# When an engine counts as free in the planner of a two-layer hybrid trunk

## The chip, the cores and the metric

The kernel runs on one core of a Trainium2 chip. The metric is the device time of one execution in microseconds (us). A core has five engines that run side by side, each through its own instructions in the order of the program: PE (TensorE, matrix products, with its weight loads, PEld), DVE (VectorE, elementwise work), ACT (ScalarE, functions and casts), POOL (GpSimd) and SP (SyncE, which here issues DMAs). They wait for one another through semaphores. So the program fixes the order on each engine, and the chip decides when each instruction runs.

## The reference

Two layers on 528 rows (512 tokens and 16 meta tokens put ahead) of 1024 features. A layer is a mixer and a feed-forward part, each with an RMS norm ahead and one behind, and a residual sum:

```python
def mixer_sublayer(h, pre_g, post_g, w_in, ...):
    u = rms_norm(h, pre_g)
    z = jnp.einsum("bld,de->ble", u, w_in)
    q, k, v, f_logit, a_val, a_gate, sc_b, sc_c, sc_x = jnp.split(z, idx, axis=-1)
    y_attn = forgetting_attention(q, k, v, log_f)          # 8 heads of 64, causal
    a = causal_depthwise_conv(a_val * sigmoid(a_gate), a_dw_w) + a_dw_b   # 31 taps
    y_conv = silu(layer_norm(a, a_ln_g, a_ln_b)) @ a_pw_w
    y_sc = sc_b * causal_depthwise_conv(sc_c * sc_x, sc_conv_w)           # 3 taps
    y = jnp.concatenate([y_attn, y_conv, y_sc], axis=-1)
    y = jnp.einsum("ble,ed->bld", head_rms_norm(y, head_g), w_out)
    return h + rms_norm(y, post_g)

def ffn_sublayer(h, pre_g, post_g, w_up, conv_w, w_down):
    z = causal_depthwise_conv(rms_norm(h, pre_g) @ w_up, conv_w)          # 3 taps
    g, up = jnp.split(z, 2, axis=-1)
    return h + rms_norm((silu(g) * up) @ w_down, post_g)
```

The feed-forward part has 2816 features inside. All is float32.

## The kernel before

Features lie on the 128 partitions, the 528 rows along the free axis, in two halves of 264. Each product of the weights is made of three matmuls of rounded parts (`mm3`, L618): high weight by high input, high by low, low by high. For it ACT casts a loaded weight block `raw` into `whi` and DVE subtracts to get `wlo` (L587 and L591 in planned code, L474 and L475 elsewhere); the inputs are split in the same way (`uhi`, `ulo`; `yhi`, `ylo`). A block has 8 slices of 128 inputs by 128 outputs, so a half of the rows needs 24 matmuls of it. The blocks are counted here in the order of use: W0 to W5 are the opening's, in mixer 0 the last are W21 (sc_x), W22 (sc_b), and then W23 and W24, the first two of w_out.

The stages, one after another: the opening (load of h, its norm, the first products), and for each layer the mixer, w_out with its post-norm, the FFN body, and ffn_down with its post-norm, behind which at the layer boundary lies the next pre-norm.

All stages but the FFN body are **planned in the source**: `Flow` (its `run` is printed below) is a list scheduler that runs while the program is built. Each piece of ACT, DVE, POOL or SP work is put in with `flow.op(engine, us, function, waits, prio)`, where `us` is a cost from a formula: `act_us(n) = 0.17 + 0.0009 n`, `dve_us(n) = 0.17 + 0.00101 n`, `stt_us(n) = 0.22 + 0.00102 n`. PE work comes from threads (generators), which count with `flow.mm(us)` and yield what they wait for. `run` keeps a clock `free[engine]` for each engine and one for PE. It always takes the piece that can start first; among those that an engine could start by then, the lowest `prio`, and then the one that was ready first. Only then is the instruction written into the program. So the times of the planner are used for nothing but the order.

The pieces of this order that matter below:

- **Norms.** Squares by ACT (L706, into `acc` or `c`), added by DVE (L715, `acc` plus `c`), summed over the partitions by PE with a constant matrix (L755, `acc` and `om_d`). ACT L765, L768, L769 and DVE L770, L776 make the factor. L797 or L1779 multiplies by it, ACT L799 or L1783 casts the result to `uhi`, DVE L800 or L1785 gives `ulo`. L832 and L842 scale the stage's output and add it to `h`. L731 is the square of the last output blocks.
- **Opening.** The first half's products run ahead of the norm (the factor comes in behind, by L893 to L901), the second half's wait for `uhi` and `ulo`.
- **Mixer.** Besides the attention (logits L1326 and L1372 with the maxima L1333, weighing L1418), DVE runs the 31 taps of the conv branch (L934). `conv_tail` (L1502 to L1546) then does its layer norm, silu and pointwise product. Each finished head block has a head norm: ACT squares, PE sums (L1100 for conv and short conv, L1484 for attention), ACT L1065, L1068, L1069, DVE L1070, L1073, L1084, then ACT L1087 `yhi` and DVE L1088 `ylo`. `conv_tail`, the projections W21 and W22 and the plain head norms take their psum banks from the ring "mm", which has two; a bank is taken again when the instructions that read it are planned as done:

```python
                ps, slot = yield from bank("mm")
                nc.tensor.matmul(ps[:, :H], lhsT=bd, rhs=sq[:, half_sl(hf)], start=True, stop=True)
                out.append(head_norm(i, yt, hf, ps[:, :H], slot, RMS_EPS, flow.mm(4 * mm_us(H))))
```

- **Early.** W23 and W24 start on those head blocks of `yhi`/`ylo` that are finished, while others are still on their way.
- **finish** does w_out or ffn_down: products in pairs of blocks, their evacuation (DVE L1610 adds the gathered product into `yp`, ACT L1613 scales it), squares, and the two norms.

## Time and profile before

| what | value |
|---|---|
| three runs, median (lowest to highest) | 1305.98 us (1305.32 to 1307.15) |
| profiled execution, its own time | 1305.24 us |
| its span | 1303.5 us |
| mean granted clock of TensorE | 0.994 |
| instructions | 24079 |
| DMA | 118.28 MB, 91 GB/s on average |

In a row of the profile stands the line of the kernel, the engine, the operation, the tile that is written and those that are read (buffer numbers left out), the shape, and a count. In a timeline the first two numbers are the start and the length, and brackets give the idle time of the engine just ahead and what ended it. In a row of a group, busy time and the mean of one instruction in ns stand behind the bar, and the idle time ahead. In a row of waits stand the total, the number of times and the longest. In a row of a window stand its length, each engine's busy time with its count of instructions (PE, PEld, DVE, ACT, POOL), the granted clock, the DMAs' share and GB/s. Matmuls are pipelined: one of 264 columns is shown 0.28 us long, and the next begins 0.12 us after it.

### The profile page before, as it was taken

The page shows a single profiled execution, that of the slowest core. Times are in us where ns is not written, and L with a number is a line of the kernel's source. Part 1 is how long each engine was busy: PE and PEld are TensorE (multiplying, and loading weights), DVE is VectorE, ACT ScalarE, POOL GpSimd, SP SyncE. Part 2 cuts the span into 40 slices and gives each one's busy share as a digit, 9 for nine tenths or more (in the row PEclk, how much of TensorE's full clock was granted, in tenths as well). Part 3 has the DMA queues.
Part 4 walks back from the last instruction along what each step waited for, and adds up shares of the span by engine and source line. Part 5 has one row for each costly group of instructions (what it writes and reads, how often), then busy time and mean ns, then how long its engine had stood idle before and what let it go on. Part 6 is the DMA issues. An engine that isn't in the chain of part 4 may idle for free. (4 is left out here: it accounts for less than half of the span.)

```text
span 1303.5 us, 24079 instructions
## 1 busy us (share of the span) xinstructions
PE 1274.5 (98%) x9922; PEld 1217.9 (93%) x9922; DVE 889.3 (68%) x1543; ACT 611.9 (47%) x1143; POOL 59.7 (5%) x166
## 2 busy tenths in 40 slices
PE   8999999999999999999989999999999999999997
PEld 8988888999999999999989898889999799989997
DVE  6888896687624663566677888856876256636664
ACT  6255567654423432344662565766543234314343
POOL 0311100000000000000003102100000000000000
PEclk8999999999999999999999999999999999999999
DMA  7133213502232223323330332234023332232221
GB/s 237 34 100 83 75 55 101 171 17 98 82 98 84 95 79 100 98 79 100 113 134 28 90 93 72 58 114 148 18 97 97 97 84 94 71 116 91 92 72 65
DMA packets 42798, 118.28 MB, mean 91 GB/s; under 512 B 4848, under 2 KB 15216, under 8 KB 42688
## 3 DMA queue, kind: packets, MB, share of 16 engines
q1 hardware_dynamic: 42640, 116.61, 28.6%
q8 instruction: 78, 1.28, 0.4%
q14 instruction: 32, 0.26, 0.1%
q0 software_dynamic: 48, 0.13, 0.0%
HBM read 108.04 MB, written 4.33 MB: 86 GB/s over the span
## 5 line engine op out<-in xcount | busy, mean ns | idle before, releaser
L618 PE MATMUL psum<-uhi,whi 128*128 128x264 f32 (+1 forms) x1936 | 453.4, 288 | 2.2 <-ACT uhi L799 1.1
L618 PE MATMUL psum<-ulo,whi 128*128 128x264 f32 (+1 forms) x1936 | 446.7, 285 | 1.0 <-DVE ulo L800 0.5
L618 PE MATMUL psum<-uhi,wlo 128*128 128x264 f32 (+1 forms) x1936 | 444.6, 283 | 0.0
L618 PEld LDWEIGHTS psum<-uhi,whi 128*128 128x128 f32 x1936 | 322.7, 189 | 4.7 <-ACT uhi L799 1.5
L618 PEld LDWEIGHTS psum<-ulo,whi 128*128 128x128 f32 x1936 | 323.9, 189 | 2.5 <-DVE ulo L800 0.7
L618 PEld LDWEIGHTS psum<-uhi,wlo 128*128 128x128 f32 x1936 | 323.5, 189 | 0.0
L618 PE MATMUL psum<-yhi,whi 128*128 128x264 f32 (+3 forms) x888 | 250.4, 305 | 7.4 <-ACT yhi L1087 2.9
L618 PE MATMUL psum<-ylo,whi 128*128 128x264 f32 (+3 forms) x888 | 247.6, 301 | 1.2 <-DVE ylo L1088 1.2
L618 PE MATMUL psum<-yhi,wlo 128*128 128x264 f32 (+3 forms) x888 | 247.3, 301 | 0.8 <-DVE wlo L591 0.8
L474 ACT CAST whi<-raw 128x1024 fp32r<-128x1024 f32 (+1 forms) x110 | 113.3, 1031 | 212.9 <-PE psum L618 199.3
L475 DVE TENSOR_TENSOR wlo<-raw,whi 128x1024 fp32r<-128x1024 f32 (+1 forms) x110 | 132.0, 1201 | 81.9 <-ACT whi L474 79.8
L618 PEld LDWEIGHTS psum<-yhi,whi 128*128 128x128 f32 x888 | 160.7, 190 | 15.7 <-ACT yhi L1087 4.3
L618 PEld LDWEIGHTS psum<-ylo,whi 128*128 128x128 f32 x888 | 161.2, 190 | 8.1 <-DVE ylo L1088 2.4
L618 PEld LDWEIGHTS psum<-yhi,wlo 128*128 128x128 f32 x888 | 161.1, 190 | 6.7 <-DVE wlo L591 1.4
L1885 DVE SCALAR_TENSOR_TENSOR c<-z,pv,c 128x528 f32<-128x528 f32 (+1 forms) x176 | 132.1, 757 | 2.7
L591 DVE TENSOR_TENSOR wlo<-raw,whi 128x1024 fp32r<-128x1024 f32 (+2 forms) x86 | 102.1, 1203 | 32.1 <-ACT whi L587 31.7
L587 ACT CAST whi<-raw 128x1024 fp32r<-128x1024 f32 (+2 forms) x86 | 87.6, 1032 | 27.1 <-PE psum L618 16.8
L934 DVE SCALAR_TENSOR_TENSOR cacc<-apad,pv,cacc 128x528 f32<-128x528 f32 x120 | 87.3, 762 | 0.8
L1903 ACT CAST yhi<-c 128x528 fp32r<-128x528 f32 (+1 forms) x44 | 27.6, 627 | 111.4 <-DVE c L1899 111.4
L1895 ACT ACTIVATE c<-c 128x528 f32<-128x528 f32 (+1 forms) x44 | 28.1, 639 | 81.8 <-DVE c L1885 81.8
L1848 DVE TENSOR_TENSOR z<-psum,rz 128x528 f32<-128x528 f32 x40 | 28.3, 708 | 53.8 <-PE psum L618 52.2
L1883 ACT ACTIVATE c<-z,pv 128x528 f32<-128x528 f32 (+1 forms) x88 | 63.3, 726 | 0.0
(214 smaller groups left out, 1364.0 us busy)
## 6 DMA issues: line engine op xcount, KB each, us to landing
raw<-in_w_dram SPq DMA_DIRECT2D x160, 512.0 KB
raw<-in_w_dram SPq DMA_DIRECT2D x32, 448.0 KB
h<-in_x_dram SPq DMA_DIRECT2D x16, 264.0 KB
raw<-in_w_dram SPq DMA_DIRECT2D x4, 528.0 KB
q<-q SPq DMA_DIRECT2D x16, 132.0 KB
k<-k SPq DMA_DIRECT2D x16, 132.0 KB
h_dram<-h SPq DMA_DIRECT2D x4, 528.0 KB
h<-h_dram SPq DMA_DIRECT2D x8, 264.0 KB
```

The costliest lines, as they stand in the source:

```text
L474: nc.scalar.copy(hi[:, :sz], raw[:, :sz])
L475: nc.vector.tensor_sub(lo[:, :sz], raw[:, :sz], hi[:, :sz].bitcast(F32))
L587: nc.scalar.copy(box["hi"][:, :sz], box["raw"][:, :sz])
L591: nc.vector.tensor_sub(lo[:, :sz], box["raw"][:, :sz], box["hi"][:, :sz].bitcast(F32))
L618: nc.tensor.matmul(d, lhsT=w[a][:, k, cols], rhs=rhs(b, k, hf), start=start and i == 0 and p == 0, stop=stop and i == n - 1 and p == 2)
L934: nc.vector.scalar_tensor_tensor(conv[j], in0=src, in1=conv[j], scalar=col("a_dw_w", CK * j + i), op0=ALU.mult, op1=ALU.add)
L1848: nc.vector.tensor_mul(two(t[:, off:]), srcs[0], two(rz))
L1883: nc.scalar.activation(dst, src[:, 2:2 + 2 * fw], AF.Copy, scale=wtap(2, t))
L1885: nc.vector.scalar_tensor_tensor(dst, in0=src[:, i:i + 2 * fw], scalar=wtap(i, t), in1=dst, op0=ALU.mult, op1=ALU.add)
L1895: silu = nc.scalar.activation(cs[0], cs[0], AF.Silu)
L1903: nc.scalar.copy(ghi, cs[0])
```

## The change

One line of `Flow.run`. After a piece is taken, its engine counts as free 0.09 us before the piece's result is there (never earlier than half its cost). The time of the result, `tok.time`, on which other pieces wait, is as before, and so is the cost of PE's work.

```diff
                 fn()
-                self.free[eng] = start + us
+                self.free[eng] = start + max(us - 0.09, 0.5 * us)
                 tok.time = start + us + lat
```

It holds for each planned engine: ACT, DVE, POOL, and SP, whose piece of 0.35 us for a DMA counts 0.26. No instruction is added or left out. What changes is the order in the planned stages: the planner sees ACT and DVE free earlier, by 0.09 for each piece since they were last idle, so that pieces change places, on PE too. Three places follow; the numbers in the names are buffer numbers.

**Opening, ACT.** The stretch from the casts of W1 and W2 to the first half's L765; the squares (L706) are those of the input `h`. Before:

```order
L587 CAST whi_224<-raw_183 128x1024
L587 CAST whi_236<-raw_191 128x1024
L706 ACTIVATE acc_243<-h_175 128x528
L706 ACTIVATE c_252<-h_175 128x528
L706 ACTIVATE c_260<-h_175 128x528
L587 CAST whi_271<-raw_208 128x1024
L706 ACTIVATE c_283<-h_175 128x528
L706 ACTIVATE acc_290<-h_175 128x528
L706 ACTIVATE c_299<-h_175 128x528
L706 ACTIVATE c_309<-h_175 128x528
L587 CAST whi_314<-raw_250 128x1024
L765 ACTIVATE rs_47_176<-psum_67,c_rms_102 128x264
```

And after:

```order
L706 ACTIVATE acc_218<-h_175 128x528
L587 CAST whi_227<-raw_183 128x1024
L587 CAST whi_238<-raw_188 128x1024
L706 ACTIVATE c_245<-h_175 128x528
L706 ACTIVATE c_254<-h_175 128x528
L706 ACTIVATE c_262<-h_175 128x528
L706 ACTIVATE acc_270<-h_175 128x528
L587 CAST whi_279<-raw_211 128x1024
L706 ACTIVATE c_288<-h_175 128x528
L706 ACTIVATE c_297<-h_175 128x528
L706 ACTIVATE c_299<-h_175 128x528
L765 ACTIVATE rs_47_176<-psum_67,c_rms_102 128x264
```

Before, the casts of W1, W2, W3 and W4 stand here, and the last square (into c) comes only behind L765. After, one square is ahead of W1, two more squares are ahead of W3, the last one is ahead of L765, and the cast of W4 has gone behind L765. On PE the first half's L755 comes behind 3 instead of 15 matmuls of W2, the second half's ahead of W3 instead of inside W4; on DVE the subtraction of W6 comes behind the second half's norm.

**End of mixer 0, DVE.** The last head norms ahead of w_out: `cacc` are the two conv head blocks, `sccx` is a short-conv head block. Before, the last twelve:

```order
L1073 SCALAR_TENSOR_TENSOR rs_t_2711<-rs_t_2711,rs_r_2710 128x264
L1084 SCALAR_TENSOR_TENSOR cacc_2544<-cacc_2544,pg_3_70,rs_t_2711 128x264
L1088 TENSOR_TENSOR ylo_293_2682<-cacc_2579,yhi_292_2681 128x264
L1088 TENSOR_TENSOR ylo_295_2694<-cacc_2544,yhi_294_2693 128x264
L1070 SCALAR_TENSOR_TENSOR rs_t_2734<-psum_67,rs_t_2734 128x264
L1073 SCALAR_TENSOR_TENSOR rs_t_2734<-rs_t_2734,rs_r_2733 128x264
L1070 SCALAR_TENSOR_TENSOR rs_t_2744<-psum_67,rs_t_2744 128x264
L1084 SCALAR_TENSOR_TENSOR cacc_2579<-cacc_2579,pg_3_70,rs_t_2734 128x264
L1073 SCALAR_TENSOR_TENSOR rs_t_2744<-rs_t_2744,rs_r_2743 128x264
L1084 SCALAR_TENSOR_TENSOR cacc_2544<-cacc_2544,pg_3_70,rs_t_2744 128x264
L1088 TENSOR_TENSOR ylo_293_2682<-cacc_2579,yhi_292_2681 128x264
L1088 TENSOR_TENSOR ylo_295_2694<-cacc_2544,yhi_294_2693 128x264
```

And after, the last ten:

```order
L1084 SCALAR_TENSOR_TENSOR cacc_2461<-cacc_2461,pg_3_70,rs_t_2625 128x264
L591 TENSOR_TENSOR wlo_2669<-raw_2207,whi_2659 128x1024
L1088 TENSOR_TENSOR ylo_288_2594<-cacc_2461,yhi_287_2593 128x264
L1070 SCALAR_TENSOR_TENSOR rs_t_2677<-psum_67,rs_t_2677 128x264
L1073 SCALAR_TENSOR_TENSOR rs_t_2677<-rs_t_2677,rs_r_2676 128x264
L1070 SCALAR_TENSOR_TENSOR rs_t_2685<-psum_67,rs_t_2685 128x264
L1084 SCALAR_TENSOR_TENSOR sccx_2158<-sccx_2158,pg_3_70,rs_t_2677 128x264
L1073 SCALAR_TENSOR_TENSOR rs_t_2685<-rs_t_2685,rs_r_2684 128x264
L1084 SCALAR_TENSOR_TENSOR sccx_2158<-sccx_2158,pg_3_70,rs_t_2685 128x264
L1088 TENSOR_TENSOR ylo_298_2664<-sccx_2158,yhi_297_2663 128x264 x2
```

Before, the two conv blocks come last; after, they are done, and the short-conv block is last. On PE the pointwise products and the conv head norms' L1100 come in front of W23 and W24, among W22's matmuls (15, 9 and 24 of them in a row), and L1100 of the short conv is last. The 31 taps end sooner on DVE, and W21 no longer runs among the maxima of the last two head pairs. Layer 1 has the same order as layer 0 now; before, it had another.

**Layer boundary, DVE.** The last pair of ffn_down of layer 0 (L1610), the second half's last square sum (L715), and the norm of the first half for layer 1. Before:

```order
L1610 TENSOR_TENSOR yp_2782<-yp_2782,psum_67 128x2x264
L770 SCALAR_TENSOR_TENSOR rz_2783<-psum_67,rz_2783 128x264
L776 SCALAR_TENSOR_TENSOR rz_2783<-rz_2783 128x264
L715 TENSOR_TENSOR acc_6985<-acc_6985,c_7329 128x528
L797 TENSOR_TENSOR yp_2782<-yp_2782,rz_2783 128x2x264 x4
L800 TENSOR_TENSOR ulo_108<-yp_2782,uhi_107 128x2x264 x2
```

And after:

```order
L770 SCALAR_TENSOR_TENSOR rz_2744<-psum_67,rz_2744 128x264
L776 SCALAR_TENSOR_TENSOR rz_2744<-rz_2744 128x264
L1610 TENSOR_TENSOR yp_2743<-yp_2743,psum_67 128x2x264
L797 TENSOR_TENSOR yp_2743<-yp_2743,rz_2744 128x2x264 x4
L715 TENSOR_TENSOR acc_6982<-acc_6982,c_7335 128x528
L800 TENSOR_TENSOR ulo_108<-yp_2743,uhi_107 128x2x264 x4
```

L1610 moves behind the factor (L770, L776), and L715 behind the four L797, which come ahead of it. On PE the L755 that reads this `acc` stands ahead of the first FFN product of the block behind, as before. In the tail of layer 1, L842 moves ahead of an L1610, and L755 of the last `acc` six matmuls forward.

## The prediction

> **What bounds the kernel now.** I read the page first (busy shares), then PE's waits, then the timelines of the places where PE waits. The page's first row and the heads of PE's list of waits:
>
> ```profile
> PE 1274.5 (98%) x9922; PEld 1217.9 (93%) x9922; DVE 889.3 (68%) x1543; ACT 611.9 (47%) x1143; POOL 59.7 (5%) x166
> ```
>
> ```profile
> PE psum L618 <- ACT yhi L1087: 2.9, 2, 1.5
> ...
> PE psum L755 <- DVE acc L715: 2.2, 1, 2.2
> PE psum L862 <- DVE yp L832: 1.4, 1, 1.4
> ```
>
> PE is busy 1274.5 of 1303.5 us, so 29 us is all that it waits in the whole span, and the change neither adds nor removes a matmul. The reader should see how little an order can win: the longest wait is 2.2 us, and most of the 29 us lies where one phase hands over to the next. What the change can do is to shift those hand-overs, in either direction. The profiled execution took 1305.24 us (span 1303.5, 1.74 around it); the three runs have a median of 1305.98, 0.74 more. I sum against the execution and add the 0.74 at the end.
>
> **Is the premise right?** The change lets the planner book an engine again 0.09 us before a result is there. Rows of the layer boundary, on DVE, then on ACT, each with the mean of one instruction of that group:
>
> ```profile
> 652.25 0.70 DVE L1610 TENSOR_TENSOR yp<-yp,psum 128x528 f32<-128x528 f32 x1 [1.22 <-PE psum L618]
> 652.87 0.42 DVE L770 SCALAR_TENSOR_TENSOR rz<-psum,rz 128x264 f32<-128x264 f32 x1
> 653.33 0.43 DVE L776 SCALAR_TENSOR_TENSOR rz<-rz 128x264 f32<-128x264 f32 x1
> 653.68 0.70 DVE L715 TENSOR_TENSOR acc<-acc,c 128x528 f32<-128x528 f32 x1
> 654.30 2.56 DVE L797 TENSOR_TENSOR yp<-yp,rz 128x528 f32<-128x528 f32 x4
> ```
>
> ```profile
> L797 DVE TENSOR_TENSOR yp<-yp,rz 128x528 f32<-128x528 f32 x8 | 5.2, 702 | 0.0
> ```
>
> ```profile
> 651.94 0.41 ACT L769 ACTIVATE rz<-rz 128x264 f32<-128x264 f32 x1
> ...
> 653.54 0.91 ACT L1613 ACTIVATE yp<-yp,pg 128x264 f32<-128x264 f32 x2
> ```
>
> ```profile
> L1613 ACT ACTIVATE yp<-yp,pg 128x264 f32<-128x264 f32 x16 | 7.5, 507 | 0.1
> ```
>
> Four L797 of 0.702 would be 2.81 one after another; they take 2.56, so each starts (2.81 − 2.56)/3 = 0.08 before the one ahead ends. Two L1613 overlap by 2 × 0.507 − 0.91 = 0.10. An instruction that reads the one ahead does not: L776 starts at 653.33, L770 ended at 653.29. So 0.09 is about the measured overlap on both engines, and results are still planned at their end. The planner's clock for a full DVE or ACT gets nearer to the chip's. But a nearer clock is no shorter chain: the instructions are the same and cost the same. The time can change only through the order, so I walk the new order by hand at the places where PE waits.
>
> **Term 1, the opening: −0.95 us.** The fence shows DVE on the way to the second half's input, and PE at its end.
>
> ```profile
> 24.33 0.43 DVE L776 SCALAR_TENSOR_TENSOR rz<-rs 128x264 f32<-128x264 f32 x1
> 24.68 1.25 DVE L591 TENSOR_TENSOR wlo<-raw,whi 128x1056 fp32r<-128x1056 f32 x1
> ...
> 27.35 0.43 DVE L770 SCALAR_TENSOR_TENSOR rs<-psum,rs 128x264 f32<-128x264 f32 x1 [0.74 <-ACT rs L769]
> ...
> 30.48 1.70 DVE L1779 SCALAR_TENSOR_TENSOR h<-h,pg,rs 128x264 f32<-128x264 f32 x4
> 32.09 0.70 DVE L1785 TENSOR_TENSOR ulo<-h,uhi 128x528 fp32r<-128x528 f32 x1
> ```
>
> ```profile
> 32.09 0.39 PE L618 MATMUL psum<-uhi,whi 128*128 128x264 f32 x1 [0.81 <-ACT uhi L1783]
> 32.85 0.39 PE L618 MATMUL psum<-ulo,whi 128*128 128x264 f32 x1 [0.37 <-DVE ulo L1785]
> ```
>
> PE has nothing from 31.28 (32.09 − 0.81), and loses 1.18. In the new order the squares go ahead of the weight casts, so that L755 of acc.0 stands 12 matmuls earlier and L755 of acc.1 27; the first half's factor (L776), at 24.76 before, can be there by about 23.4; the weight subtraction of 24.68 (1.25 long, 1.17 with the overlap) goes behind the norm. From 24.68 to 32.09 DVE takes 7.4 us, 0.9 of it idle. Without the subtraction, and with five more L1779 (1.61 from 30.48 to the next start, by four: 0.40 each) pulled ahead of the first ulo, that is 7.4 − 0.9 − 1.2 + 2.0 = 7.3: the first ulo could start at 23.4 + 7.3 = 30.7. I add 0.45 because L893 must wait for its product, so 31.15, and PE gets it 0.75 later, at 31.9 instead of 32.85. Gain 0.95; at most the 1.18 that is lost now, and nothing if L893 waits 1.4 longer than I think.
>
> **Term 2, the end of each mixer: +0.8 and +0.4 us.** This is the largest and least certain term. Before, the conv branch's head norms come last, and w_out waits for them. PE over the last part of mixer 0 as a window, then PE's waits in it, and two spacings after the same wait in layer 1:
>
> ```profile
> 170.55:222.66 52.11, 48.32 (x360) 42.70 (x359) 40.92 (x109) 36.42 (x101) 3.44 (x14) 1.00 0.26 83
> ```
>
> ```profile
> 216.70 0.39 PE L618 MATMUL psum<-ylo,whi 128*128 128x264 f32 x1 [0.39 <-DVE ylo L1088]
> ...
> 219.87 0.51 PE L618 MATMUL psum<-yhi,whi 128*128 128x264 f32 x2 [1.47 <-ACT yhi L1087]
> 220.64 0.39 PE L618 MATMUL psum<-ylo,whi 128*128 128x264 f32 x1 [0.26 <-DVE ylo L1088]
> ...
> 222.66 0.39 PE L618 MATMUL psum<-yhi,whi 128*128 128x264 f32 x1 [0.54 <-ACT acc L706]
> ```
>
> ```profile
> 868.45 0.61 PE L618 MATMUL psum<-yhi,whi 128*128 128x250 f32 x2 [1.47 <-ACT yhi L1087]
> 869.23 0.57 PE L618 MATMUL psum<-ylo,whi 128*128 128x250 f32 x1 [0.16 <-DVE ylo L1088]
> 869.60 0.41 PE L618 MATMUL psum<-yhi,wlo 128*128 128x250 f32 x1
> 869.81 0.41 PE L618 MATMUL psum<-ylo,whi 128*128 128x250 f32 x1
> ```
>
> Four waits, 0.39 + 1.47 + 0.26 + 0.54 = 2.66, stand at the end of mixer 0. They go: taps are done earlier on DVE, so conv_tail runs earlier, and the short-conv norms are last, behind the early products of w_out's first two blocks (W23, W24). But conv_tail, the sc_x and sc_b blocks (W21, W22) and the plain head norms all take their psum from the two "mm" banks, and now they come one behind another. A bank that a norm holds is free only when L1065, L1068, L1069 and L1070 are through:
>
> ```profile
> 216.91 0.48 ACT L1065 ACTIVATE rs_r<-psum,c_rms 128x264 f32<-128x264 f32 x1
> ...
> 217.60 0.41 ACT L1068 ACTIVATE rs_r<-rs_r 128x264 f32<-128x264 f32 x1
> 218.04 0.42 ACT L1069 ACTIVATE rs_t<-rs_r 128x264 f32<-128x264 f32 x1
> ```
>
> 0.48 + 0.41 + 0.42 and 0.43 for L1070 are 1.74, with four hand-overs of 0.05 some 1.95 us, in which PE has 9 to 15 matmuls of 0.12 (1.1 to 1.8 us) of W22 for cover at best, and sometimes a bank is missing for W22 itself. My walk finds new waits of 0.8 (the first pointwise product behind the silu chain), 1.9 (the fourth behind the copy that frees its bank, itself behind a weight cast on ACT), 2.7 (two L1100 and W22's second half behind the norms' banks) and 0.6 (W23 behind L1012): 6.0. It takes away the 2.66, about 2.0 in which lone norm matmuls stand wide apart (inside PE's busy time, so no row gives it), and 0.5 in the chain of the attention maxima: 5.2. Net +0.8 in layer 0. After the change layer 1 has layer 0's order; before, it lost 0.6 more than layer 0, because the matmuls from 869.60 on stand 0.21 apart where 0.12 is usual; so +0.4 there. The bounds: if the new waits are half as long, −2.2 and −2.6; if each of the four is a half longer, +3 each.
>
> **Term 3, the layer boundary: +0.55 us.** In the new DVE order L1610 goes behind L770 and L776, and L715 (acc with the last c) from ahead of the four L797 to behind them, while PE still has L755 of that acc ahead of the first FFN block. PE's rows:
>
> ```profile
> 654.44 1.16 PE L755 MATMUL psum<-acc,om_d 128*128 128x264 f32 x4 [2.23 <-DVE acc L715]
> 656.69 0.39 PE L618 MATMUL psum<-uhi,whi 128*128 128x264 f32 x1 [1.09 <-ACT uhi L799]
> 657.53 0.59 PE L618 MATMUL psum<-ulo,whi 128*128 128x264 f32 x1 [0.46 <-DVE ulo L800]
> 657.92 0.42 PE L618 MATMUL psum<-uhi,wlo 128*128 128x264 f32 x1
> 658.14 0.42 PE L618 MATMUL psum<-uhi,whi 128*128 128x264 f32 x1
> ...
> 660.34 0.34 PE L618 MATMUL psum<-ulo,whi 128*128 128x264 f32 x1
> ```
>
> L770 now comes first and starts at 652.38, since its factor by L769 ends at 652.35, L776 at 652.84, L1610 at 653.19, the L797 from 653.77 to 656.33, L715 to 656.95. PE's L755 goes at 657.05 instead of 654.44. Before, that L755 lay under the L797 and cost nothing; now it is in front of the first block, which starts at 657.95. Its third matmul comes at 658.4 where it came at 657.92: about +0.5. The idle time is one piece of 4.8, 652.21 (654.44 − 2.23) to 657.05, in place of 2.23 + 1.09 + 0.46. Already now the matmuls from 657.53 to 660.34 stand 0.22 apart instead of 0.12; that lasts to 3.65 us after 656.69. The same 3.65 from 657.05 ends at 660.7: +0.05 more. Bounds: 0 (L755 is done under the ulo) and +2 (the wide spacing lasts 13 matmuls longer, 13 × 0.1, and the 0.5).
> The Trainium skill, TensorE: Matmul & The Clock Gate, Part 1: The HAM clock gate, has the PE clock halved after an idle window of about 3.4 us and restored after as much busy time. The rows of the boundary agree (2.23 + 1.09 + 0.46 idle, 0.22 apart for 2.8 us). By that rule the 4.8 us in one piece costs what I put, and a bank wait of 1.9 costs no clock; but at 868.45 a single 1.47 was followed by the wide spacing, and in layer 0 the same 1.47 was not. So the rule alone does not settle the third rival below.
>
> **Costed at nothing.** In w_out and ffn_down casts and squares trade places, and PE has no wait there that these pieces end; if that cover went, each instruction that comes too late would show with its lateness. In the tail L842 goes ahead of L1610 and L755 of acc.15 six matmuls earlier (0.7 us): the input of its second part, c by L731, ends at 1288.71 (row below), and PE, which comes to it at 1289.56 now, at 1288.86, so no wait; the last chain, behind the last block's products, is unchanged.
>
> ```profile
> 1288.29 0.42 ACT L731 ACTIVATE c<-yp 128x256 f32<-128x256 f32 x1 [0.64 <-DVE yp L1632]
> ...
> 1289.56 0.59 PE L755 MATMUL psum<-c,om_d 128*128 128x256 f32 x2
> ```
>
> SP's loads and POOL's memsets swap by a place or a few; the loads run far ahead of use. Bounds for all this: −0.5 to +0.5.
>
> **Sum.** −0.95 + 0.8 + 0.4 + 0.55 + 0 = +0.8: 1306.0 for such an execution, 1306.8 with the 0.74 to the median. A measurement tells about 0.2% (2.6 us) from no change.
>
> **Rivals.**
> *The banks do not bind* (chance 0.27). The conv branch finishes early, as the DVE rows intend, and half the 6.0 of new waits is hidden: mixers −2.2 and −2.6, the rest as above: 0.8 − 1.2 − 4.8 = −5.2 to the execution, 1300.8. For it: 2.66 is at stake in rows, and DVE is 40.92 of 52.11 busy in the window, so it has room. Against it: only two banks, and a holding time near 2 us each.
> *Slower through PE's clock* (0.28). The bank waits come in pieces long enough that the matmuls behind them stand 0.22 apart, 13 of them at each mixer end (13 × 0.1 = 1.3, as from 869.60 on), and the boundary's 4.8 us adds its further 1.5: 1306.8 + 1.3 + 1.3 + 1.5 = 1310.9. It decides once a wait before w_out is over about 1.5 us. For it: layer 1 shows it after 1.47. Against it: layer 0 does not.
> *Nothing comes through* (0.12). PE is 98% busy; the moved instructions are under its cover, and gains and losses are each under a microsecond: 1306.0.
> My forecast has the rest, 0.33, with its own range of 1304.5 to 1309.
>
> **How the numbers follow.** Faster by over 0.2% (under 1303.4) holds nearly all of the first rival and a little of the forecast: 0.27. Slower (over 1308.6) holds most of the second and the forecast's upper end: 0.30. The rest, 0.43, is within. The range reaches to the first rival's 1300.8 less 0.8, and to the second's 1310.9 plus 0.6: 1300 to 1311.5 leaves about a tenth on each side.
>
> **What would show it.** Opening: PE's wait for uhi L1783 and ulo L1785 of 1.18 falls to about 0.3. Mixers: no wait for yhi L1087 of the conv norm just before w_out, but waits of L1100, L1531's followers and W22 for L1070 or for L1546's copy. Boundary: one wait of L755 for acc L715 of about 4.8 us. The prediction is wrong if PE's list of waits shows under 3 us of bank waits in both mixers together (then the first rival), or if the granted clock falls at the mixer ends (the second). It would be wrong in its premise if the FFN body, which is not planned, changed by more than 0.3 us.

## The result: 1.5% slower, and where the time went

| kernel | median, us (lowest to highest) | ratio to before, 95% interval |
|---|---|---|
| before | 1306.05 (1305.32 to 1307.15) | |
| after | 1326.26 (1324.57 to 1327.81) | 1.015 (1.0137 to 1.0164) |

The forecast was 1306.8, its range 1300 to 1311.5. The change costs 20.2 us. In the profiled execution the span is 22.3 us longer, 1325.8 in place of 1303.5. The page's first row after the change:

```profile
PE 1286.5 (97%) x9922; PEld 1225.4 (92%) x9922; DVE 887.0 (67%) x1543; ACT 611.4 (46%) x1143; POOL 58.9 (4%) x166
```

The work is the same. PE is shown 12 us busier because a matmul at a lower clock is shown longer (0.42 instead of 0.29 us in the rows below). So the busy row hides half of the loss, and I compared the stages by milestones instead: the starts, in PE's timeline, of matmuls that occur once or in few groups. "Attention part" runs from the sums of the forget gate (L1211) to the fourth and last weighing (L1418), "mixer's end" from there to the first square sum behind w_out (L755). That L755 shifts by a few matmuls between orders, so a difference under half a microsecond means nothing, and one at a mixer's end holds up to 1 us of it (8 matmuls in layer 0).

| stage | before, us | after, us | difference | forecast |
|---|---|---|---|---|
| start to L1211 of mixer 0 | 72.0 | 69.9 | −2.1 | −0.95 |
| attention part, layer 0 | 120.1 | 127.1 | +7.0 | 0 |
| mixer's end, layer 0 | 57.2 | 63.3 | +6.1 | +0.8 |
| first w_out and FFN, layer 0 | 386.4 | 389.0 | +2.6 | 0 |
| layer boundary to L1211 of mixer 1 | 82.6 | 83.1 | +0.5 | +0.55 |
| attention part, layer 1 | 121.0 | 123.7 | +2.7 | 0 |
| mixer's end, layer 1 | 58.3 | 63.8 | +5.4 | +0.4 |
| second w_out, FFN, to the tail | 379.3 | 379.3 | 0 | 0 |

Almost all of it lies in the two mixers: 9.7 in their attention parts and 11.5 at their ends. The border between the two is not firm, since the new order moves work across it: after the change 18 and 15 fewer matmuls of L618 stand in the attention parts, and 24 and 21 more at the ends. At 0.12 us each this is an estimate of what equal work costs more: 9.2 and 4.5 in the attention parts, 3.2 and 2.9 at the ends. The whole mixers are 13.1 and 8.1 us longer. The waits of PE after the change, the longest ones and what answers to those shown of before:

```profile
PE psum L1100 <- DVE rs_t L1070: 4.1, 2, 2.0
PE psum L755 <- DVE acc L715: 4.1, 1, 4.1
PE psum L1326 <- ACT yta L1448: 3.6, 2, 2.2
PE psum L618 <- DVE wlo L591: 2.5, 3, 1.0
...
PE psum L862 <- DVE yp L832: 1.4, 1, 1.4
...
PE psum L1100 <- DVE sccx L1012: 1.2, 2, 0.6
```

The wait for the conv norm's yhi (L1087) is gone, as forecast, and norm sums (L1100) that wait for a bank to be freed by L1070 are new, as forecast too. The L1326 that wait for L1448 are new, and I did not foresee them: they stand in the attention part.

**Mixer's end.** PE where the two conv norms queue:

```profile
211.39 0.29 PE L618 MATMUL psum<-uhi,wlo 128*128 128x264 f32 x1
212.30 1.13 PE L1100 MATMUL psum<-apad,bd 128*128 128x264 f32 x4 [0.61 <-DVE sccx L1012]
215.46 1.25 PE L1100 MATMUL psum<-apad,bd 128*128 128x264 f32 x2 [2.04 <-DVE rs_t L1070]
216.27 0.66 PE L618 MATMUL psum<-uhi,whi 128*128 128x264 f32 x1
216.73 0.42 PE L618 MATMUL psum<-ulo,whi 128*128 128x264 f32 x1
216.95 0.42 PE L618 MATMUL psum<-uhi,wlo 128*128 128x264 f32 x1
```

Between 211.39 and 216.27 the PE gets three norm sums done. Behind the wait the next matmuls stand 0.22 apart instead of 0.12: the clock had fallen. Its granted value, the third number from the right, in three windows of 5 us:

```profile
140.00:145.00 5.00, 5.00 (x32) 4.84 (x31) 3.27 (x10) 0.71 (x2) 0.00 (x0) 0.67 0.31 102
190.00:195.00 5.00, 5.00 (x27) 4.83 (x28) 4.28 (x13) 2.22 (x6) 1.43 (x4) 0.66 0.00 0
215.00:220.00 5.00, 4.54 (x24) 4.23 (x25) 3.97 (x10) 2.83 (x8) 0.00 (x0) 0.66 0.00 0
```

Each such window loses about a third of 5 us, 1.7 us; before, no window of mixer 0 was below 1.00. Over all 5 us windows up to PE's last matmul, what the clock lacks to 1.00 sums to 11.9 us after and 6.9 before, 5.0 of the 22 us. By stage the difference is larger in the mixers: 8.5 after and 1.7 before in the two of them together, while the opening lacked 3.4 before and nothing after. This bounds what the clock can have cost, since it also counts time in which PE waits.

**Attention part.** DVE in the middle of it, after:

```profile
112.80 0.44 DVE L1333 CUSTOM_DVE_ANT_0 junk<-psum,causal 128x272 bf16<-128x272 f32 x1
...
113.16 0.77 DVE L934 SCALAR_TENSOR_TENSOR cacc<-apad,pv,cacc 128x528 f32<-128x528 f32 x1
113.85 0.57 DVE L1333 CUSTOM_DVE_ANT_0 junk<-psum,causal 128x400 bf16<-128x400 f32 x1
...
114.56 0.43 DVE L1333 CUSTOM_DVE_ANT_0 junk<-psum,causal 128x264 bf16<-128x264 f32 x1
...
117.18 0.77 DVE L934 SCALAR_TENSOR_TENSOR cacc<-apad,pv,cacc 128x528 f32<-128x528 f32 x1
117.86 0.43 DVE L1073 SCALAR_TENSOR_TENSOR rs_t<-rs_t,rs_r 128x264 f32<-128x264 f32 x1
118.21 0.77 DVE L934 SCALAR_TENSOR_TENSOR cacc<-apad,pv,cacc 128x528 f32<-128x528 f32 x1
...
126.61 2.45 DVE L591 TENSOR_TENSOR wlo<-raw,whi 128x1024 fp32r<-128x1024 f32 x2
...
132.28 1.22 DVE L591 TENSOR_TENSOR wlo<-raw,whi 128x1024 fp32r<-128x1024 f32 x1
```

Taps of the conv branch (L934) stand among the maxima and the factors of the head norms. The subtraction of W15 comes at 126.61 and that of W17 at 132.28; before they came at 115.98 and 128.65:

```profile
115.98 1.22 DVE L591 TENSOR_TENSOR wlo<-raw,whi 128x1024 fp32r<-128x1024 f32 x1
...
128.65 1.22 DVE L591 TENSOR_TENSOR wlo<-raw,whi 128x1024 fp32r<-128x1024 f32 x1
```

A subtraction frees one of three buffers into which later weights are loaded, and SP issues the loads in order. Two of the three are held by W18 and W19, which are loaded and not yet cast, so the load of the conv branch's pointwise weight (the first of four in these rows) can go only when W17's subtraction is through. SP's queue after, then before:

```profile
133.53 29.05 SPq L583 DMA_DIRECT2D raw<-in_w_dram  x4
```

```profile
129.89 25.29 SPq L583 DMA_DIRECT2D raw<-in_w_dram  x4
```

So this weight lands later, and ACT, whose next instruction is its cast, waits 6.01 us for that transfer (4.16 before), with the evacuation of a weighing (L1445 to L1449) behind it. ACT after, then before:

```profile
137.12 0.62 ACT L587 CAST pw<-raw 128x512 fp32r<-128x512 f32 x1 [6.01 <-DMA raw<-in_w_dram]
137.65 0.59 ACT L1445 ACTIVATE s<-psum 128x512 f32<-128x512 f32 x1
...
138.69 0.18 ACT L1448 COPY yta<-psum 128x16 f32<-128x16 f32 x1
```

```profile
132.58 0.62 ACT L587 CAST pw<-raw 128x512 fp32r<-128x512 f32 x1 [4.16 <-DMA raw<-in_w_dram]
```

PE needs the bank that L1448 frees. It has no such wait before. Its row after:

```profile
138.93 0.50 PE L1326 MATMUL psum<-k,q 128*128 128x144 f32 x2 [2.23 <-ACT yta L1448]
```

And the early taps brought nothing. The last one before started at 171.52, the last one after at 142.45, yet conv_tail's first product starts later. The last tap and conv_tail after, then before:

```profile
142.45 0.76 DVE L934 SCALAR_TENSOR_TENSOR cacc<-apad,pv,cacc 128x528 f32<-128x528 f32 x1
```

```profile
182.01 1.94 PE L1502 MATMUL psum<-cacc,om_c 128*128 128x264 f32 x8
```

```profile
171.52 0.76 DVE L934 SCALAR_TENSOR_TENSOR cacc<-apad,pv,cacc 128x528 f32<-128x528 f32 x1
```

```profile
174.21 0.61 PE L1502 MATMUL psum<-cacc,om_c 128*128 128x264 f32 x2
```

The thread of conv_tail is started at its own place in the list of projections (`fill`), right behind the second sc_c block (W19), whose last matmul is at 181.88. The finished taps lay 39 us.

A switch in the program decides where the taps go: of 31 taps a block, the first 25 have priority 4, the last `LATE = 6` have 0.5, ahead of head norms (1) and weight subtractions (2).

```python
            for i in range(CK):
                for j in range(2):
                    last[j] = dve(stt_us(L), lambda j=j, i=i: tap(j, i), last[j], prio=4 if i < CK - LATE else 0.5)
```

The planner's own clock (numbers of the program, not of the chip) has the first tap of priority 0.5 at 153 us in the kernel before and at 104 us in the changed one, since a DVE that is free 0.09 us earlier after each instruction takes a tap into more gaps. With the cut on DVE alone it is 121, so the cut on ACT has its part in it. Below, "late taps from" is this number.

### The profile page after: what moved, and what is told of

It reads as the page before. It is cut to its first block, busy times and chain, and to the rows that moved or that the text cites. A ratio compares the mean times of both kernels' runs of the same rounds, so it can differ in the third digit from the quotient of the medians.

```text
span 1325.8 us, 24082 instructions
## 1 busy us (share of the span) xinstructions
PE 1286.5 (97%) x9922; PEld 1225.4 (92%) x9922; DVE 887.0 (67%) x1543; ACT 611.4 (46%) x1143; POOL 58.9 (4%) x166
## 5 line engine op out<-in xcount | busy, mean ns | idle before, releaser
L618 PE MATMUL psum<-uhi,whi 128*128 128x264 f32 (+1 forms) x1936 | 460.0, 290 | 2.2 <-DVE rs_t L1070 1.0
L618 PE MATMUL psum<-ulo,whi 128*128 128x264 f32 (+1 forms) x1936 | 452.1, 286 | 0.9 <-DVE ulo L1785 0.6
L618 PE MATMUL psum<-uhi,wlo 128*128 128x264 f32 (+1 forms) x1936 | 449.9, 284 | 0.0
L618 PEld LDWEIGHTS psum<-uhi,whi 128*128 128x128 f32 x1936 | 326.5, 190 | 5.3 <-DVE rs_t L1070 1.9
L618 PEld LDWEIGHTS psum<-ulo,whi 128*128 128x128 f32 x1936 | 327.4, 190 | 2.2 <-DVE ulo L1785 0.8
L618 PEld LDWEIGHTS psum<-uhi,wlo 128*128 128x128 f32 x1936 | 327.0, 190 | 0.0
L618 PE MATMUL psum<-yhi,whi 128*128 128x264 f32 (+3 forms) x888 | 249.1, 303 | 3.7 <-ACT whi L587 2.3
L618 PE MATMUL psum<-yhi,wlo 128*128 128x264 f32 (+3 forms) x888 | 246.4, 300 | 2.5 <-DVE wlo L591 2.5
L618 PE MATMUL psum<-ylo,whi 128*128 128x264 f32 (+3 forms) x888 | 245.9, 299 | 0.0
L618 PEld LDWEIGHTS psum<-yhi,whi 128*128 128x128 f32 x888 | 160.1, 189 | 11.1 <-ACT whi L587 3.0
L618 PEld LDWEIGHTS psum<-yhi,wlo 128*128 128x128 f32 x888 | 160.0, 189 | 8.5 <-DVE wlo L591 3.2
L618 PEld LDWEIGHTS psum<-ylo,whi 128*128 128x128 f32 x888 | 160.3, 189 | 5.5
L934 DVE SCALAR_TENSOR_TENSOR cacc<-apad,pv,cacc 128x528 f32<-128x528 f32 x120 | 87.2, 762 | 0.7
L1848 DVE TENSOR_TENSOR z<-psum,rz 128x528 f32<-128x528 f32 x40 | 28.3, 707 | 52.9 <-PE psum L618 51.4
L1883 ACT ACTIVATE c<-z,pv 128x528 f32<-128x528 f32 (+1 forms) x88 | 63.3, 726 | 0.4 <-DVE z L1851 0.4
```

Of the source, the lines that this page charges most:

```text
L618: nc.tensor.matmul(d, lhsT=w[a][:, k, cols], rhs=rhs(b, k, hf), start=start and i == 0 and p == 0, stop=stop and i == n - 1 and p == 2)
L934: nc.vector.scalar_tensor_tensor(conv[j], in0=src, in1=conv[j], scalar=col("a_dw_w", CK * j + i), op0=ALU.mult, op1=ALU.add)
L1848: nc.vector.tensor_mul(two(t[:, off:]), srcs[0], two(rz))
L1883: nc.scalar.activation(dst, src[:, 2:2 + 2 * fw], AF.Copy, scale=wtap(2, t))
```

## The experiments

The theories by their letters, as the expectations use them: A, the cut on DVE is to blame (A', because some lines of DVE get an early start that they do not have); B, the cut on ACT; C, the order of SP's loads; D, the rival to all, that any change of the planner's numbers spoils a finely fitted order; E, the late taps; F, the queue for two psum banks at the mixers' ends, my forecast's own mechanism; G, E and F together.

The kernels differ from the one before in the lines shown. Where there is no diff of the planner's line, it is that of the change. All times are medians in us; before was 1305.9 to 1306.6 beside them.

### One engine at a time, and one stage at a time

```diff
-                self.free[eng] = start + us
+                self.free[eng] = start + (max(us - 0.09, 0.5 * us) if eng == "dve" else us)
```

e1_dve is this; e2_act has `eng == "act"`, e3_sp_pool `eng in ("sp", "pool")`, and in e4_outside the condition is a flag that is off while a mixer is planned.

> The cut of 0.09 for DVE alone; ACT, POOL and SP are planned as before. Theory A (the planner runs ahead of the chip on DVE: it puts low-priority taps and square sums into DVE time that isn't there, so the attention chain and the weight subtractions come late, and with them loads): most of the 20 us comes from DVE, 1318 to 1328 us, and a mixer longer by over 6 us. Theory B (the cut on ACT is what hurts): within 3 us of before. Theory C (SP's loads trading places with the q and k copies hurts): within 5 us of before. Theory D (any small change of the planner's numbers throws a finely fitted order off): 1310 to 1325 as for the other engines.

> The cut for ACT alone. Theory A: within 5 us of before (1301 to 1311), since ACT is busy 47% and seldom the engine that is waited for. Theory B: 1316 to 1326. Theory C: within 5 us. Theory D: 1310 to 1325.

> The cut for SP and POOL alone. Theory A and B: within 2 us of before. Theory C: a large part of the 20 us, 1314 to 1324, with the load of the pointwise weight landing some 4 us later than before. Theory D: 1308 to 1320.

> The cut on all engines, but not while the two mixers are planned: it holds in the opening, in w_out and in ffn_down with their norms. Theory A: the mixers as before, the opening 1.4 us faster, w_out and the boundary slower by up to 3.5: 1303 to 1309. Theory D: the order of the mixers starts from another state and is thrown off all the same, 1310 to 1320. If the loss lies outside the mixers, 1318 or more.

Measured: DVE alone 1305.24, ratio 0.9991 (0.998 to 1.0002); ACT alone 1308.9, 1.0022 (1.001 to 1.0033); SP and POOL alone 1306.19, 1.0001 (0.999 to 1.0013); outside the mixers 1306.14, 0.9997 (0.9986 to 1.0008). Theory A, that the cut on DVE is to blame by itself, fell at once: it costs nothing. B and C fell as well, though ACT alone costs 3.0 us, with an end of mixer 0 of 65.8 us. The loss needs the mixers, and no engine alone gives it. In e4_outside the stage from the first w_out on was 389.1, as after the change: that 2.6 belongs to the cut in w_out, and the opening's gain sets off part of it. D had its first counts against it: three changes of the planner in four cost nothing.

### Both engines, mixers alone, and the late taps

f3_dve_act and f4_mixers are the condition `eng in ("dve", "act")` and the flag the other way round. The other two touch only the switch:

```diff
 # f1_late0: the change, and
-LATE = 6
+LATE = 0
 # f2_before_late: no change of the planner, and
-LATE = 6
+LATE = 15
```

> The changed kernel (cut on every engine), but with LATE = 0: the last six taps of each conv block keep priority 4 and never rank ahead of a head norm (1) or a weight subtraction (2). Theory E (the cut makes the taps run ahead in the plan, so that their last six, of priority 0.5, reach the attention chain some 55 us sooner and push the weight subtractions W15 to W17 and the head norms back): 1304 to 1312. Theory D (any change of the planner's numbers costs): 1315 to 1330. Theory C (loads behind the q and k copies): 1320 to 1330.

> The kernel before, without any cut, but LATE = 15, so that priority 0.5 begins at the same place of the attention chain as in the changed kernel (the planner's 101 us; 104 in the changed kernel, 153 before). Theory E: slower by 6 to 20 us, 1312 to 1326, without any cut. Theories A, B: within 4 us of before. Theory D: 1310 to 1325 too, so only f1 tells E from D.

> The cut for DVE and ACT together, SP and POOL planned as before. If SP's order is part of the loss (theory C, in company with the others): under 1318. Theory E: the taps reach priority 0.5 at the same place (the planner's 104 us), so 1322 to 1330.

> The cut on every engine, only while the two mixers are planned, the complement of the run outside the mixers. If the stages add up: 1326. Theory E: the planner reaches priority 0.5 at 116 us, between the changed kernel (104) and the cut on DVE alone (121, 1305): between 1305 and 1326, some 1315.

Measured: f1 1319.87, 1.0104 (1.0075 to 1.0134); f2 1324.1, 1.0137 (1.0107 to 1.0166); f3 1326.36, 1.0154 (1.0124 to 1.0183); f4 1324.71, 1.0141 (1.0112 to 1.0171). DVE and ACT together are the whole loss, though each alone is none or little of it. f2 costs 18 us with no cut at all: its late taps begin at 101, and nine more taps of each block have the priority. Its attention parts are 125.4 and 125.8, its ends 64.0 and 63.8. But it is not the changed kernel's loss over again: PE has no wait of L1326 for L1448 in it, waits longest for L1012 (5.1 in two waits), and its granted clock is 0.56, 0.50 and 0.58 in the three windows from 125 to 140 us. f1 gave back only 6.4, which lies in D's range and not in E's: its attention parts fell to 123.4 and 122.6, its ends stayed long (63.6 and 61.3). In f1 the subtraction of W15 is back at 117.0, yet that of W17 comes at 132.6, ACT still waits 5.83 for the pointwise weight and PE 2.04 for L1448. So the last six taps are not what delays that load; what does is open. Theory E, the late taps, is at most half of an answer, and the mixers' ends are another matter. f4 came out longer than my guess, near the sum of the stages (1326).

### Other banks for the head norms, and truer costs

```diff
 # g1_cut_acc (with the change) and g2_acc (without), in plain_head_norm
-                ps, slot = yield from bank("mm")
+                ps, slot = yield from bank("acc")
                 nc.tensor.matmul(ps[:, :H], lhsT=bd, rhs=sq[:, half_sl(hf)], start=True, stop=True)
```

In h1_exempt the cut does not hold for the 64-partition subtractions and the maxima, which I took to have no early start on the chip (for the maxima the trace bears this out only where another maximum follows, see the last section): for `eng == "dve"` and the pieces of L1259, L1287 and L1333 the engine is booked for `us + 0.04`. g3_cut03 has 0.03 in place of 0.09.

> The changed kernel, but the plain head norms (L1100) take their psum bank from the ring acc, which is idle after the last weighing, instead of mm. Theory F (the mixer's end is longer by some 6 us in each layer because conv_tail, W22 and the norms queue for two mm banks, and PE's clock falls behind the waits): 1313 to 1319, with the waits of L1100 for L1070 (4.1 us now) under 1 us. If the banks are not the cause of the mixer's end: 1322 to 1330. The attention part stays as in the changed kernel in both.

> The kernel before, without a cut, with the same other ring for the head norms. Theory F: its norms come behind the first blocks of w_out and do not queue in front of W22, so little changes, 1303 to 1308. It is also the yardstick for the run before it.

> The cut on every engine, except on three lines of DVE whose next instruction does not start early on the chip: the 64-partition subtractions L1259 and L1287 (next start 0.03 us after the end) and the maxima L1333 (some 0.2 us after): those count 0.04 us more than their cost. Theory A' (the plan is too early for DVE in the attention part because these 200 instructions get a cut that they do not have, so taps are squeezed in ahead of time that is not there): the attention part as long as before, 1306 to 1315, the taps' priority 0.5 from the planner's 132 us on. Theory D (any change throws the order off): 1315 to 1330.

> A cut of 0.03 instead of 0.09 on every engine. Theories A', E and F, by size: the plan runs ahead by a third as much, so 1306 to 1313. Theory D: as likely 1315 to 1325 as less, with no order by size.

Measured: g1 1311.19, 1.0039 (1.0019 to 1.0058); g2 1299.29, 0.9946 (0.9923 to 0.9968); h1 1299.59, 0.9944 (0.9922 to 0.9967); g3 1305.32, 0.9992 (0.9981 to 1.0004). With another ring the mixers' ends are 57.6 and 56.7, as before or shorter; the attention parts stay at 124.2 and 123.7. PE's waits of g1 have no L1100 any more, and what is left of the bank queue is this row:

```profile
PE psum L618 <- DVE rs_t L1070: 0.9, 2, 0.5
```

So the queue for two banks is shown as a cause at the ends: 63.3 − 57.6 and 63.8 − 56.7, 12.8 us in both, with the same 399 matmuls of L618 in each end, and the time fell by 15.1, below the range of theory F. The norms' other ring alone also beats the kernel before by 6.8 us, which I had not expected; its whole mixers are 2.3 and 4.4 us shorter than before. Against this yardstick the change costs 11.9 us with the other ring, in place of 20.2: its ends are 57.6 and 56.7 against 56.0 and 57.8, with 21 and 6 more matmuls of L618 in them, its attention parts 124.2 and 123.7 against 119.1 and 117.1. So the queue makes some 8 of the 20 us by this comparison, and the attention parts stay long although in g1 PE has no wait for L1448 and ACT waits only 1.21 for the pointwise weight. The chain of rows shown above is thus one form that the loss takes there, not the whole of its cause. g3 cost nothing, where I had expected up to 7 us. h1 came out faster than before, with everything in the mixers short (119.7 and 119.5, 56.1 and 56.0), which looked like a proof for truer costs.

### Is it the truth of the costs?

k1_only3 cuts only those three lines; k2_cost3 cuts nothing and books only those three lines for `us + 0.04`. k3_exempt_acc is h1 with the other ring; k4_best is k3 with the cut only in the opening and the mixers.

> The cut of 0.09 on the three lines L1259, L1287 and L1333 alone. Theory A' (these lines count less than they take on the chip, and the attention part pays): slower than before, 1309 to 1318, with the attention part (L1211 to the fourth L1418) over 2 us longer than before in mixer 0. If the three lines are not the cause: 1303 to 1308.

> No cut; the three lines count 0.04 us more than before, nearer to what they take. Theory A': as fast as with the cut and the exemption, 1297 to 1303, since the attention part gains from their true cost. If the gain of h1_exempt came from the cut on the other lines (or from the luck of an order): 1304 to 1309.

> The cut with the three lines exempt (h1_exempt, 1299.6), and the head norms on the ring acc (alone 1299.3). If both gains are of different places: 1291 to 1296. If both act on the mixers' ends, which h1_exempt has already at 56 us: 1298 to 1302.

> The run beside it, with the cut only in the opening and the mixers; w_out, ffn_down and the layer boundary are planned as before. If the 2.6 us of the first w_out and the 1.2 us of the boundary belong to the cut there: 3 to 4 us less than the run beside it. If they come with the state that the mixers leave behind: within 1.5 us of it.

Measured: k1 1311.22, 1.0039 (1.0023 to 1.0055); k2 1323.86, 1.0134 (1.0114 to 1.0154); k3 1298.78, 0.9942 (0.9922 to 0.9962); k4 1297.39, 0.9931 (0.9914 to 0.9948). k1 came out as A' has it, in time and in the length of the attention part. k2 did not, and lies in neither range: it loses 17 us. It is not the truer plan that I took it for: in the trace of before, the next instruction starts behind L1259 on average 0.02 us later than the plan's cost has it, behind L1287 at the cost, and behind L1333 0.03 earlier (pairs more than 0.2 us apart left out), so 0.04 more is no nearer for any of them. Its attention parts are short (119.6 and 119.4) and its ends are the longest of all (68.1 and 67.7): its late taps come from 162 on and conv_tail starts at 194.8, so that w_out waits for the conv heads, and its ends also lack 6.8 and 5.1 us of clock. PE in k2:

```profile
211.72 0.39 PE L618 MATMUL psum<-yhi,whi 128*128 128x264 f32 x1 [3.98 <-ACT yhi L1087]
```

That is the opposite fault to the changed kernel's. By this reading h1 was fast because its late taps begin at 132, between the two; no run tests that by itself. k3 came out as expected for gains that both act on the mixers' ends. k4 is the fastest kernel of the study, 9.3 us under the runs of before beside it. Its stage from the first w_out on is 386.3 where k3 has 389.0, so the 2.6 us are the cut's in that stage, though only 1.4 of it arrive in the time, since the boundary is 1.1 longer (83.0 against 81.9).

### Moving only the taps

```diff
+                self.free[eng] = start + (us + 0.1 if <a tap> else max(us - 0.09, 0.5 * us))
```

n1_taps is the change with the taps alone counted longer, which brings the late taps to 131; n2_taps_acc has the other ring too.

> The cut on every engine as in the changed kernel, but a conv tap (L934) counts 0.1 us more than its cost instead of 0.09 less, so that the taps reach priority 0.5 at the planner's 131 us instead of 104. Theory G (where the taps fall decides the attention part, the two banks the end): the attention part (L1211 to the fourth L1418) as before within 1.5 us, the mixers' ends as long as in the changed kernel if the norms still queue: 1312 to 1319. If the place of the taps is not the cause: 1322 or more.

> The run beside it, with the head norms on the ring acc as well. Theory G: both losses gone, what stays is the first w_out and the boundary (3.8) less the opening's gain: 1298 to 1306. If something else than taps and banks makes up the 20 us: 1310 or more (the other ring alone gave 1311.2).

Measured: n1 1313.89, 1.0056 (1.0034 to 1.0079); n2 1302.74, 0.9975 (0.9963 to 0.9986). In n1 the attention parts are 119.0 and 119.8, 8.1 and 3.9 shorter than after the change, with the same work in them but for one block of three matmuls. That is no longer than before, although at equal work (21 and 18 fewer L618 than before, at 0.12) it would be 1.4 and 1.0 longer by estimate. The ends stay at 63.8 and 62.9. The list of PE's waits of n1 begins like that of the changed kernel, but without L1326 for L1448:

```profile
PE psum L1100 <- DVE rs_t L1070: 4.1, 2, 2.0
PE psum L755 <- DVE acc L715: 4.1, 1, 4.1
PE psum L618 <- DVE wlo L591: 2.8, 3, 1.0
```

ACT's cast of the pointwise weight now stands behind L1449 and waits 0.88:

```profile
131.63 0.63 ACT L1449 COPY yta<-psum 128x512 f32<-128x512 f32 x1
133.15 0.62 ACT L587 CAST pw<-raw 128x512 fp32r<-128x512 f32 x1 [0.88 <-DMA raw<-in_w_dram]
```

In n2 the ends fall to 55.0 and 56.7 as well. Both expectations held. The change with both mends takes 1326.3 less 12.4 (n1) less 11.2 more (n2). The two do not simply add: with the other ring put in first, the banks take 15.1 and the taps 8.5. And since the ring gives 6.8 without the change too, the fair yardstick for n2 is g2: n2 is 3.5 us slower, and 2.6 of that is the first w_out, which n2 also has (389.0). So taps and banks together account for 16.7 of the 20.2 us, by the medians: some 8 to 12 for the taps and 4 to 8 for the banks, depending on which is mended first.

Over the runs, by the place of the late taps in the plan:

| run | late taps from | attention part, layers 0 and 1 | mixer's end, 0 and 1 | whole mixer, 0 and 1 |
|---|---|---|---|---|
| f1_late0 | none | 123.4, 122.6 | 63.6, 61.3 | 187.0, 183.9 |
| f2_before_late | 101 | 125.4, 125.8 | 64.0, 63.8 | 189.4, 189.6 |
| after | 104 | 127.1, 123.7 | 63.3, 63.8 | 190.4, 187.4 |
| f3_dve_act | 104 | 124.1, 123.7 | 63.4, 63.8 | 187.6, 187.5 |
| f4_mixers | 116 | 126.7, 123.6 | 62.8, 64.2 | 189.5, 187.8 |
| e1_dve | 121 | 122.1, 121.8 | 57.8, 58.0 | 179.9, 179.8 |
| n1_taps | 131 | 119.0, 119.8 | 63.8, 62.9 | 182.7, 182.8 |
| h1_exempt | 132 | 119.7, 119.5 | 56.1, 56.0 | 175.8, 175.6 |
| k1_only3 | 135 | 123.1, 126.7 | 57.6, 55.7 | 180.7, 182.4 |
| g3_cut03 | 137 | 120.9, 121.5 | 57.4, 56.1 | 178.3, 177.6 |
| e4_outside | 148 | 120.1, 120.8 | 57.3, 58.0 | 177.4, 178.8 |
| before | 153 | 120.1, 121.0 | 57.2, 58.3 | 177.3, 179.3 |
| e3_sp_pool | 153 | 120.2, 121.0 | 57.2, 58.5 | 177.4, 179.5 |
| e2_act | 160 | 121.3, 120.0 | 65.8, 57.7 | 187.1, 177.7 |
| k2_cost3 | 162 | 119.6, 119.4 | 68.1, 67.7 | 187.7, 187.1 |
| other ring: g1_cut_acc | 104 | 124.2, 123.7 | 57.6, 56.7 | 181.8, 180.4 |
| other ring: k3_exempt_acc | 127 | 121.5, 121.5 | 53.5, 53.6 | 175.0, 175.2 |
| other ring: k4_best | 127 | 121.6, 121.5 | 53.9, 53.7 | 175.5, 175.1 |
| other ring: n2_taps_acc | 127 | 122.1, 119.4 | 55.0, 56.7 | 177.1, 176.1 |
| other ring: g2_acc | 147 | 119.1, 117.1 | 56.0, 57.8 | 175.0, 174.9 |

The place is that of layer 0. Since work moves between the two parts, only the last column compares like with like. From 121 to 153 a mixer takes 176 to 183 us; up to 116, and at 160 and above, 187 to 190 (in e2_act in layer 0 alone). Where it is late the end pays. Where it is early the attention part pays, and the end is long too. k1_only3 looks like an exception, with long attention parts at 135: 15 and 30 more matmuls of L618 than before stand in them, 1.8 and 3.6 us by estimate, and its whole mixers are some 3 us longer than before. f1_late0 is an exception: it has no late taps and its mixers are 184 to 187. The place of the taps also does not decide whether the norms queue for banks; n1 and h1 differ there at the same place. So the table shows a connection over many orders, and n1 alone moves the taps with the rest of the change kept. Theory D does not hold as it is worded: e1, e3, e4 and g3 cost nothing, and h1 is faster than before.

## Why the prediction was wrong, step by step

**What bounds it** was read rightly: the change adds no work, and what it moved is hand-overs. But I took the list of waits as the size of what is at stake ("29 us is all that it waits"). That caps what an order can win. It says nothing about what an order can lose.

**The premise** ("The planner's clock for a full DVE or ACT gets nearer to the chip's") failed as a step. Two pairs of rows showed an overlap of 0.08 and 0.10, and I carried them over to all instructions. For the sum over a stage the old booking was nearly right: in mixer 0 before, the planner's start of the weight subtractions W12 to W21 is within 0.5 us of the trace's (115.98 on the chip, 116.08 in the plan for W15); further on the chip is ahead of that plan, by 1.5 at W22 and 6.5 at W27. After the change the chip is 2.9 us behind the plan at W12, 6.9 at W15 and 8.9 at W21. Part of that is the change's own stalls. Part is that some pairs were given an early start that they do not have: the maximum at 113.85 in the fence above is 0.57 long and the next one starts 0.71 behind its start, and L1259 on 64 partitions, 0.43 long, is followed 0.44 to 0.46 behind its start. How the 8.9 divide is not shown. Whether a truer plan would be faster is open too: k1 and h1 fit that, but no run has costs that are nearer to the chip throughout. My own sign for the premise, the unplanned FFN body, held for its main part: from its first product with w_down to the first square sum of ffn_down it takes 280.35 us before and after. Where it joins on w_out, PE has new waits for z (L1848, 0.45 us).

**Term 1, the opening**, was right in kind: PE's waits there fell, and the first matmul of W6, the next block, came 1.42 earlier where I had 0.95. PE after, at the hand-over:

```profile
31.27 0.39 PE L618 MATMUL psum<-ulo,whi 128*128 128x264 f32 x1 [0.62 <-DVE ulo L1785]
```

The waits of 1.18 became 0.62, where I had 0.3, and the first matmul of the second half starts at 30.36 instead of 32.09. The −2.1 of the table is partly chance: in the profiled execution of before the granted clock was 0.50 from 10 to 15 us, and 1.00 in that of after. Over the profiled executions with the cut in the opening (after, f1, g1, e4) L1211 comes at 69.9 to 71.2, over those without (before, f2, f4, g2, k2) at 71.0 to 72.0; the means differ by 0.8.

**Term 2, the mixers' ends**: the mechanism was right and the size was off, +0.8 and +0.4 against +6.1 and +5.4, or against about 3 each at equal work. (By the prediction's own 0.6 between the layers the second figure should have been +0.2.) The waits for the conv norm went, and the waits of L1100 and W22 for banks came. The new waits were smaller than the 6.0 that I had: in rows of PE 0.53, 0.30, 0.61 and 2.04 in layer 0, 3.5 in all. The mis-sized part is what I took away against them, 5.2. Only the 2.66 that stood in rows were there to take. The "about 2.0 in which lone norm matmuls stand wide apart" had no row and did not go away: the eight L1100 sums of mixer 0 hold PE for 5.56 us after, 4.65 before. A weight subtraction that comes late for W26 cost 1.0 more, and the granted clock, 1.00 throughout this stage before, lacks 1.7 us in it after. PE's idle time in the stage rose by 1.9 us, which with at most 1.7 for the clock covers the 3.2 at equal work. g1 takes the queue away and gains 12.8 us in both layers, more than the change had cost there, since the ring helps the kernel before as well. I took the net of two nearly equal sums of hand-made terms, and the error of each was larger than the net.

**The attention part** is the step that failed outright: it stands in the sum with nothing but a gain of 0.5 "in the chain of the attention maxima", and it measured +7.0 and +2.7 us. "They go: taps are done earlier on DVE, so conv_tail runs earlier" holds a cause without its price, and its effect was not so. The taps stand in DVE's time ahead of maxima, head norms and weight subtractions; booked longer in n1, they give back 12.0 us of the attention parts. Conv_tail did not run earlier, since its thread waits for its place in `fill`. Which of the displaced instructions costs how much is not shown: after the change the rows lead to the load of the pointwise weight, in g1 and f2 the attention parts are long too (124.2 and 125.4 in layer 0) without that wait. I followed where the taps ended, not what they now stood in front of, and did not read the priorities: 0.5 for the last six. "The loads run far ahead of use" was wrong at one place: the load of the pointwise weight was already late before (ACT waited 4.16 for it).

**Term 3, the boundary**, was right in kind and nearly in size: one wait of 4.06 us for L715, forecast 4.8, and from the last product of ffn_down to the second FFN pair 1.1 us more, forecast 0.55; by the milestones +0.5, since part comes back. PE after:

```profile
669.98 2.13 PE L755 MATMUL psum<-acc,om_d 128*128 128x264 f32 x4 [4.06 <-DVE acc L715]
671.53 0.79 PE L618 MATMUL psum<-uhi,whi 128*128 128x264 f32 x1
672.12 0.42 PE L618 MATMUL psum<-ulo,whi 128*128 128x264 f32 x1
```

The first sums at half the clock (2.13 for what took 1.16) make up for the shorter wait.

**Costed at nothing**: the tail was right (0). The first w_out was not, at 2.6: with the cut off there it is gone (k4 against k3), in the second w_out it never appeared, and why is open.

**The rivals**: the second one's clock is there, with a lack of 5.1 us at the two ends after the change against 1.7 before, where the rival had 1.3 each; it had named the right sign, a fall of the clock at the mixer ends, and missed the attention part like the rest. "The banks do not bind" is refuted by g1 under this order. None of the four cases came near 1326, since all priced the same places and none the attention part.

## What to carry to other kernels

In a list scheduler with priorities a small change of costs is not a small change of order. Moving the costs by 0.03 to 0.1 us moved a batch of low-value work ahead of or behind the chain beside it, and with the same instructions the result lay between 0.6% faster (h1) and 1.5% slower; before judging a change of costs, list where each class of work lands against the chain that it can delay, and against what waits for it. Where several stages take buffers from one small ring, look for the ring that is idle at that time: here one word gave 0.5% by itself and took 15 of the 20 us back, 8 of them beyond what it gives without the change. When two orders are compared by stages, count the work in each stage: here some 20 matmuls had moved across the border, and 2 to 3 us with them. When the order of everything changes, a net of hand-made terms is worth less than the larger of its errors, and the range has to say so.

## What the runs showed of the hardware

On DVE an instruction that does not read the one ahead can start about 0.08 us before that one's recorded end (the four L797 of the prediction), on ACT 0.10 us (its two L1613); one that reads it starts 0.03 to 0.04 us behind. It depends on the pair. Behind a maximum of L1333 another maximum starts some 0.15 us after the end (113.85 and 0.57 long, next at 114.56), but a tap starts 0.08 us early (the maximum of 112.80 ends at 113.24, the tap starts at 113.16); so it is behind 40 of the 96 maxima after the change. Behind L1259 on 64 partitions every next instruction starts 0.01 to 0.03 us after the end or later.

PE's clock fell to half for about 3.4 us (windows of 5 us at 0.66 and 0.67) around waits of 2.23 and 2.04 us in the changed kernel. The fall at 190 to 195 came with no such wait, only 0.42, 0.21 and 0.48 us one behind another:

```profile
188.60 0.43 PE L1350 MATMUL psum<-ident_r,mcol 16*1 16x16 f32 x4 [0.42 <-DVE mcol L1333]
189.25 0.22 PE L1350 MATMUL psum<-ident_r,mcol 128*1 128x128 f32 x1 [0.21 <-DVE mcol L1333]
189.94 0.39 PE L618 MATMUL psum<-uhi,whi 128*128 128x264 f32 x1 [0.48 <-DVE rs_t L1070]
```

In the kernel before, a wait of 1.47 was followed by it in layer 1 and not in layer 0. In f2 the clock was at 0.50 to 0.58 through the three windows from 125 to 140 us, although PE was busy 4.3 to 5.0 us in each. The Trainium skill (TensorE: Matmul & The Clock Gate, Part 1) puts an idle window of about 3.4 us ahead of the lower clock; the lower clock's own length agrees with it in the windows of the changed kernel, but shorter waits than that were enough.
